# More Strassen pairs in an MLP's down projection, their weight-block sums made by DMA in two quarters of the residual

## The chip, the cores and the metric

The kernel runs on one core of a Trainium2 chip. Its time is the device time of one execution in microseconds (us); the figure compared is the median over several executions. One execution is also recorded by the hardware profiler, and its trace is what the views below are taken from.

## The reference

One block of an encoder, batch 1, 256 rows, width 2048, in float32. Four kinds of mixers, an output projection and a cross-attention stand ahead of the part that matters here:

```python
D_MODEL = 2048
SEQ = 256
D_FF = ((8 * D_MODEL // 3 + 255) // 256) * 256        # 5632

def swiglu(h, w_gate_up, w_down):
    gate, up = jnp.split(h @ w_gate_up, 2, axis=-1)
    return (jax.nn.silu(gate) * up) @ w_down

def reference(x, mem, norm_g, ...):
    ...
    for l in range(DEPTH):                             # DEPTH is 1
        ...
        x = x + mix @ w_out[l]
        x = x + cross_attention(rms_norm(x, norm_g[l, 1]), mem_n, w_xq[l], w_xkv[l], w_xo[l])
        x = x + swiglu(rms_norm(x, norm_g[l, 2]), w_gate_up[l], w_down[l])
    return rms_norm(x, final_norm_g)
```

## The kernel before

**Products.** Every float32 operand is held as two parts, hi and lo. A product of 128 rows of activations with a block row of 512 weight columns is three matmuls on TensorE (PE), hi with wh (L472), hi with wl (L473) and lo with wh (L474), all in `part`.

**Weights.** They stream from HBM in slabs of 16 blocks of 128x128, 1 MB each (`Stream`). `_load` reads a slab into one of three raw buffers; ScalarE (ACT) rounds a half of it to wh (L166, or L178 in a pair), and VectorE (DVE) subtracts to get wl (L167, L179). The halves lie in a ring of split buffers: three, with one more (`wy`) in the MLP, and another (`wz`) in most of gate_up. So Down has four, and a cast waits until PE has used up the half four places earlier. GpSimd (POOL) and SyncE (SP) issue DMAs. The order of these steps on ACT and DVE is fixed in the program by the order in which they are written (`add_manual_dep` in `_half`).

**Plain slabs and pairs.** The MLP's slabs go by plans, strings with one letter a slab. N is a plain slab: four steps of 512 columns, two row halves each, 24 matmuls. S and s are pairs: two k-blocks and two groups of 512 columns, in which Strassen's form does with seven products what takes eight, 21 matmuls. A pair needs sums of activations (`combine`, nine VectorE operations, and casts by ScalarE), and sums of the four weight blocks. The split is then made in four phases (`_sums`): a block pair, a single block, a block pair, a block pair. In a pair of kind s, VectorE makes the sums of weight blocks in the raw buffer with four operations of 128x512 between the second phase and the third (L189). In a pair of kind S, two of them are made by DMA: SP reads 256 KB into a tile t (L114), ScalarE copies it into t's second half (L119), and POOL adds 512 KB from HBM to t by an accumulating DMA (L121); VectorE then makes only two sums, and the raw buffer reads only 768 KB. The tiles t are the four quarters of the residual `res`, whose rows lie in HBM in the meantime (`leave`) and are read back at the end of gate_up. In the code before, only gate_up has pairs of kind S with DMA sums; Down writes S in its plans too, but its slabs aren't in `SUMMED`, so that they are made as s.

**gate_up** is a first group of columns without pairs and ten groups of eight slabs each (`GROUPS`). After every group, silu(gate) times up is stored to HBM by POOL (`hidden<-g`, L600) and read back turned (`tmp<-hidden`, L605); ScalarE and VectorE split it to the activations f[0] to f[43] of Down (`fetch`). 22 of them are fetched during gate_up, the others at its end and in Down.

**Down** runs two passes of 22 slabs (`PASSES`), each for two groups of 512 columns; the last three slabs of pass 2 (`LATE`) are held for `down_end`, which finishes the last columns and the final norm. `mixed` adds the four banks of the pairs to the residual when the last pair of a pass is done. `paired_rows` works the plain steps in the order of k, those in `soon` first; `ready(k)` makes sure that f[k] is there, with the number of tiles to be had rising by three in four steps; `before(j)` makes sure that the combine of the pair at j is there. Otherwise fetches and combines are written into the program from a queue (`Background`), by a modelled time of PE and VectorE.

Of the kernel before, what the change touches and what calls it, by code (L numbers as in the profile page):

```python
# [19 lines left out]
ALU = mybir.AluOpType  # L20
# [8 lines left out]
FT = DFF // P  # L29
# [10 lines left out]
ROWS = ((0, 512), (704, 1024), (1088, NBLK))  # L40

LATE = 12

GATE_UP = 1920 // 16 + 8
GROUPS = *["NSSNSSNN"] * 9, "NSNSNSNN"

DOWN = GATE_UP + 80
PASSES = "NNNNNSNNSNNSNSNNSNNSNN", "NSNSNSNSNSNSNSNSNSNNNN"

PAIRED = {a + i for a, plan in [(GATE_UP + 8 * j, GROUPS[j % len(GROUPS)]) for j in range(10)] + [(DOWN, PASSES[0]), (DOWN + 22, PASSES[1])]  # L50
          for i, x in enumerate(plan) if x in "Ss"}
AHEAD = (-3, -3)

SUMS = [{GATE_UP + 8 * j + i + a: GATE_UP + 8 * j + i for j in range(10) for i, x in enumerate(GROUPS[j % len(GROUPS)]) if x == "S"}
        for a in AHEAD]

SUMMED = {GATE_UP + 8 * j + i for j in range(10) for i, x in enumerate(GROUPS[j % len(GROUPS)]) if x == "S"}

LAG, OWED, SOON, FAR = 1.3, 0.9, 0.01, 18.0
V_NG = 0  # L60
# [16 lines left out]
class Stream:  # L77


    def __init__(self, tc, pools, W, bg):  # L80
        self.tc, self.nc, self.W, self.bg = tc, tc.nc, W, bg
        self.rawp, self.wp = pools
        self.order = []
        self.n = self.made = 0
        self.after = []
        self.halves = []
        self.at = self.phase = 0
        self.raw = None
        self.ring = [[self.wp, -1] for _ in range(3)]
        self.last = {}  # L90
        self.raws = [[self.rawp, -1] for _ in range(3)]
        self.sums = []
        self.places = []
        self.two = []
        self.begun = []

    def _buffers(self, n, m):

# [6 lines left out]
    def _load(self, n):  # L105

        nc = self.nc
        slot = min(self.raws, key=lambda x: x[1])
        slot[1] = n
        self.raw = slot[0].tile([P, 2048], F32, name="raw", tag="raw")  # L110
        if n // 16 in SUMS[0]:
            t = self.sums[0]
            self.sums.append(self.sums.pop(0))
            nc.sync.dma_start(t[:, 0:512], self.W[SUMS[0][n // 16]][:, 1536:2048])  # L114
            self.begun.append(t)
        if n // 16 in SUMS[1]:
            t = self.begun.pop(0)
            mark = len(nc.cur_bb.bb.instructions)
            nc.scalar.copy(t[:, 512:1024], t[:, 0:512])  # L119
            self.keep(mark)  # L120
            nc.gpsimd.dma_start(t, self.W[SUMS[1][n // 16]][:, 512:1536], accum_op=ALU.add)  # L121
            self.two.append(t)
        if n // 16 in SUMMED:
            nc.sync.dma_start(self.raw[:, 0:1536], self.W[n // 16][:, 0:1536])
            return
        for a, b in zip(CUTS[n], CUTS[n][1:]) if n in CUTS else [(0, 1024), (1024, 2048)] if self.after else [(0, 2048)]:
            (nc.scalar if (n, a) == (0, 0) else nc.sync).dma_start(self.raw[:, a:b], self.W[n // 16][:, a:b])
            if self.after:
                self.after.pop(0)()

    def _half(self):
# [5 lines left out]
        mark = len(ins)  # L137
        (self._sums if n // 16 in PAIRED else self._plain)()
        if n // 16 < GATE_UP - 12:
# [31 lines left out]
    def _sums(self):  # L171

        nc, r, ph = self.nc, self.raw, self.phase
        summed = self.made // 16 in SUMMED
        t = self.two and self.two[0]
# [55 lines left out]
    def take_sums(self, w, ks, cols):  # L231

        assert self.n // 16 in PAIRED and self.n % 16 == 0
        self.order += [(w, ks[k], cols[c] + i * P) for k, c in ((1, 0), (0, 0), (1, 1), (0, 1)) for i in range(4)]
# [58 lines left out]
class Block:  # L293
# [563 lines left out]
    def whole(self, c):  # L857
        return self.res[c].rearrange("p k r -> p (k r)")

    def leave(self, c):  # L860
        self.nc.sync.dma_start(self.rd[:, c * 1024:(c + 1) * 1024], self.whole(c))

# [237 lines left out]
    def gate_up(self, gp, f, z):  # L1100

        nc = self.nc
        box, g, stored = {}, {}, []
# [36 lines left out]
        def fetch(k0, k1, ahead, pause, after=0, slow=False):  # L1140

            m = {}
            for k in range(k0, k1 + ahead):
                if k < k1:
                    while len(stored) <= k // 4:
                        yield
                    while after and self.bg.now < stored[k // 4] + after:
                        yield
                    m[k] = self.tmp()
                    mark = self.mark()  # L1150
                    self.load_turned(m[k], self.ff, k)
                    self.keep_place(mark)
                    if slow and k < k0 + ahead - 1:
                        yield
                if k >= k0 + ahead:
                    while k0 == 0 and k - ahead >= 20 and "free" not in box:
                        yield
                    mark = self.mark()
                    self.split(f[k - ahead], m.pop(k - ahead))
                    self.keep_place(mark)  # L1160
                    self.have = k - ahead + 1
                    yield pause
# [21 lines left out]
        sums = [((2 * i, 2 * i + 1), z[(i + 1) % 4]) for i in range(4)]  # L1184
        comb = self.bg.add(combined())
        whole = [self.whole(c) for c in range(4)]
# [17 lines left out]
        self.st.raws.append([rx, -1])  # L1204
        gate(ps[0])
        up(0, ps[1])
        early = fetch(0, FT - 22, 2, 2.0, 12, True)
        self.bg.drain(comb)
        for j in range(1, DFF // 512):
            plan = GROUPS[(j - 1) % len(GROUPS)]  # L1210
            if j == 10:
                box["free"] = True
            turns = [i for i, x in enumerate(plan) if x == "N"][:3]
            if j == 10:
                rest = fetch(FT - 22, FT, 6, SOON, slow=True)

            def begin(i):

                if (j, i) == (10, 5):
                    self.st.back(self.wz, rx)  # L1220
                if i in turns:
                    next(early, None)
                if j == 10 and i > 2:
                    next(rest)

            upped(j, self.paired_rows("w_gate_up", [j * 512, DFF + j * 512], self.h3, sums[:8 - plan.count("N")], plan, mixed, gated,
                                      before=begin, swap=j % 2 == 0)[0])
        more.close()
        for c, x in enumerate(whole):
            nc.sync.dma_start(x, self.rd[:, c * 1024:(c + 1) * 1024])  # L1230
        for _ in early:
            pass
        self.fetch = self.bg.add(rest)
# [1 line left out]
    def down(self, f, sp):  # L1235
# [4 lines left out]
        nc, st = self.nc, self.st  # L1240
        ss = self.rp.tile([P, 24], F32, name="rc", tag="rc")
        self.gap(sp, 192)
        z = [sp.tile([P, 768], F32R, name=f"y{i}") for i in range(8)]
        u = sp.tile([P, 512], F32, name="u")
        sums = [((2 * i, 2 * i + 1), z[i % 8]) for i in range(PASSES[1].count("S"))]
        made, split = [], []

        def combined(n):
# [36 lines left out]
        asked = itertools.count(1)  # L1285

        def ready(k):

            need = min(FT, max(k + 3, FT - 22 + next(asked) * 3 // 4))
            while self.have < need:  # L1290
                self.bg.step(next(e for e in self.bg.q if e[0] is self.fetch))

        for i, plan in enumerate(PASSES):
            n = plan.count("S")
            g = self.bg.add(combined(n))
            late = (0, LATE)[i]
            plan = plan[:22 - late // 4]

            def before(j):
                while plan[j] == "S" and len(made) <= plan[:j].count("S"):  # L1300
                    self.bg.step(next(e for e in self.bg.q if e[0] is g))
                if late and j == len(plan) - 2:
                    st.back(self.wy)

            ps, rest = self.paired_rows("w_down", [2 * i * 512, (2 * i + 1) * 512], f, sums[:n], plan,
                                        lambda *q: mixed(2 * i, *q), lambda *q: done(2 * i, *q), ready, late, before, i == 1,
                                        () if i else range(2 * n, 2 * n + 8))
            if i == 0:
                done(1, *ps)
        return ss, ps, rest, split  # L1310
# [316 lines left out]
class Gla:  # L1627
# [31 lines left out]
    def fetch(self):  # L1659

        b = self.b
        for to, k in ((self.k, 2), (self.q, 0)):
            for hd in range(4):
                c = (k + hd // 2) * R
                src = b.gq[c:c + R, :].rearrange("(g f) (b t) -> (f b) g t", f=32, t=32)[hd % 2 * 64:hd % 2 * 64 + 64]
                for d in (0, 64):
                    b.nc.gpsimd.dma_start(to[d:d + 64, hd, :].rearrange("p (g t) -> p g t", t=32), src)
# [324 lines left out]
```

## Time and profile before

| | us |
|---|---|
| median of 3 runs | 1429.03 |
| fastest, slowest | 1428.62, 1430.32 |
| the profiled execution | 1428.43 |
| its span | 1426.6 |
| outside the span | 1.8 |
| Down starts (first f tile in a matmul) | about 1186 |
| pass 2 starts | about 1301 |

Line numbers in the views are those of the kernel before. PE is TensorE's matmuls, PEld its weight loads, DVE is VectorE, ACT ScalarE, POOL GpSimd, SP SyncE. A row of a timeline gives start, duration, engine, line, operation, output<-inputs with shapes and the number of operations put together (x); in brackets the idle time before it, and what ended it. A row of waits gives who waited for whom: total us, times, longest. The granted clock of TensorE was 0.999 over the span, so that nothing here is a matter of its throttle.

### The profile page before, as it was taken

How to read it: one execution, taken by the hardware profiler on the slowest of the kernel's cores; microseconds unless marked ns; L12 is line 12 of the kernel's file. 1: busy time of each engine (PE TensorE's matmuls, PEld its weight loads, DVE VectorE, ACT ScalarE, POOL GpSimd, SP SyncE). 2: the span in 40 equal slices, each digit the busy share in tenths (PEclk: the TensorE clock that was granted, in tenths of full speed). 3: DMA queues.
4: the chain of work that ended last, by engine and by line, in shares of the span. 5: the costliest groups of instructions: out<-in, count | busy, mean ns of one | idle time of the engine just before them, and what ended most of it. 6: DMA issues, size and time to landing. Idle time of an engine off the chain costs nothing.

```text
span 1426.6 us, 18663 instructions
## 1 busy us (share of the span) xinstructions
PE 1416.5 (99%) x6562; PEld 1176.1 (82%) x6562; DVE 1174.3 (82%) x1782; ACT 850.2 (60%) x1242; POOL 243.4 (17%) x315
## 2 busy tenths in 40 slices
PE   9999999999999999999999999999999999999997
PEld 8888888888888888888888888888888888788886
DVE  6667868787878767677578999999999988989997
ACT  7566665445755555555465676667666665655655
POOL 0000100003212233531331121122211024000000
PEclk9999999999999999999999999999999999999999
DMA  9886554457566797965798999999999898665554
GB/s 356 294 291 250 204 198 174 161 177 232 183 216 215 234 278 249 276 197 188 252 298 257 265 280 283 288 291 260 278 291 273 276 276 242 212 235 179 193 220 148
DMA packets 72462, 344.84 MB, mean 242 GB/s; under 512 B 10894, under 2 KB 12591, under 8 KB 45745
## 3 DMA queue, kind: packets, MB, share of 16 engines
q1 hardware_dynamic: 52976, 285.31, 57.4%
q0 software_dynamic: 18960, 57.69, 17.2%
q8 instruction: 51, 0.84, 0.2%
q10 hardware_dynamic: 432, 0.66, 0.1%
q14 instruction: 43, 0.34, 0.1%
HBM read 321.07 MB, written 22.54 MB: 241 GB/s over the span
## 4 chain that ended last, share of the span: by engine, by line
PE 92%; issue 3%; DVE 2%; DMA 2%; POOL 1%; ACT 0%; SPq 0%; DVEq 0%; ACTq 0%; POOLq 0%
PE pg L472 21%; PE pg L474 21%; PE pg L473 21%; PE pm L473 6%; PE pm L474 6%; PE pm L472 6%; PE pg L420 4%; PE pg L421 2%; PE pm L1445 1%; DMA raw<-in_W 1%; PE pm L1074 1%; DMA tmp<-hidden 1%; POOL tmp L605 1%; PE pm L1045 1%; DVE wl L179 0%
## 5 line engine op out<-in xcount | busy, mean ns | idle before, releaser
L167 DVE TENSOR_TENSOR wl<-raw,wh 128x1024 fp32r<-128x1024 f32 (+1 forms) x395 | 473.7, 1212 | 161.3 <-ACT wh L166 159.4
L166 ACT CAST wh<-raw 128x1024 fp32r<-128x1024 f32 (+1 forms) x395 | 406.4, 1042 | 253.0 <-PE pg L474 189.0
L472 PE MATMUL pg<-wh,act 128*128 128x512 f32 (+1 forms) x1165 | 455.5, 391 | 0.0
L474 PE MATMUL pg<-wh,act 128*128 128x512 f32 (+1 forms) x1165 | 453.9, 390 | 0.5 <-DVE act L322 0.5
L473 PE MATMUL pg<-wl,act 128*128 128x512 f32 (+1 forms) x1165 | 453.6, 389 | 0.2 <-DVE wl L167 0.2
L474 PEld LDWEIGHTS pg<-wh,act 128*128 128x128 f32 x1165 | 218.9, 188 | 47.0 <-DVE act L322 1.1
L472 PEld LDWEIGHTS pg<-wh,act 128*128 128x128 f32 x1165 | 219.0, 188 | 46.8 <-issue 1.5
L473 PEld LDWEIGHTS pg<-wl,act 128*128 128x128 f32 x1165 | 219.0, 188 | 45.1 <-DVE wl L167 0.5
L178 ACT CAST wh<-raw 128x1024 fp32r<-128x1024 f32 (+1 forms) x177 | 161.5, 918 | 158.8 <-DVE raw L189 62.7
L179 DVE TENSOR_TENSOR wl<-raw,wh 128x1024 fp32r<-128x1024 f32 (+1 forms) x177 | 182.7, 1057 | 25.7 <-ACT wh L178 24.3
L473 PE MATMUL pm<-wl,act 128*128 128x512 f32 x290 | 112.9, 389 | 0.2 <-DVE wl L167 0.2
L472 PE MATMUL pm<-wh,act 128*128 128x512 f32 x290 | 112.8, 389 | 0.0
L474 PE MATMUL pm<-wh,act 128*128 128x512 f32 x290 | 112.8, 389 | 0.0
L420 PE MATMUL pg<-act,wh 128*128 128x512 f32 x256 | 90.5, 395 | 0.0
L121 POOL DMA_DIRECT2D res<-in_W x39 | 35.0, 897 | 238.3 <-ACT res L119 211.1
L421 PE MATMUL pg<-act,wl 128*128 128x256 f32 x256 | 71.8, 280 | 0.0
L189 DVE TENSOR_TENSOR raw<-raw 128x512 f32<-128x512 f32 x99 | 68.2, 689 | 1.6
L473 PEld LDWEIGHTS pm<-wl,act 128*128 128x128 f32 x290 | 54.4, 188 | 11.8 <-DVE wl L167 0.5
L474 PEld LDWEIGHTS pm<-wh,act 128*128 128x128 f32 x290 | 54.4, 188 | 11.3
L472 PEld LDWEIGHTS pm<-wh,act 128*128 128x128 f32 x290 | 54.4, 188 | 11.3
L420 PEld LDWEIGHTS pg<-act,wh 128*128 128x128 f32 x256 | 48.1, 188 | 10.5
L178 ACT CAST wh<-res 128x1024 fp32r<-128x1024 f32 x39 | 41.2, 1055 | 14.8 <-PE pg L474 4.1
(376 smaller groups left out, 1933.0 us busy)
## 6 DMA issues: line engine op xcount, KB each, us to landing
raw<-in_W SPq DMA_DIRECT2D x207, 1024.0 KB, 5.5
raw<-in_W SPq DMA_DIRECT2D x39, 768.0 KB, 8.9
res<-in_W POOLq DMA_DIRECT2D x39, 512.0 KB, 9.7
res<-in_W SPq DMA_DIRECT2D x39, 256.0 KB, 4.9
raw<-in_W SPq DMA_DIRECT2D x11, 512.0 KB, 7.1
hidden<-g POOLq DMA_DIRECT2D x22, 256.0 KB, 4.0
tmp<-hidden POOLq DMA_DIRECT2D x44, 128.0 KB, 10.5
features<-tmp POOLq DMA_DIRECT2D x32, 128.0 KB, 4.6
```

Of the source, the lines that this page charges most:

```text
L121: nc.gpsimd.dma_start(t, self.W[SUMS[1][n // 16]][:, 512:1536], accum_op=ALU.add)
L166: nc.scalar.copy(wh[:, a:b], r[:, a:b])
L167: nc.vector.tensor_tensor(out=wl[:, a:b], in0=r[:, a:b], in1=wh[:, a:b].bitcast(F32), op=ALU.subtract)
L178: nc.scalar.copy(wh, src)
L179: nc.vector.tensor_tensor(out=wl, in0=src, in1=wh.bitcast(F32), op=ALU.subtract)
L189: nc.vector.tensor_tensor(out=out, in0=a, in1=b, op=ALU.add)
L420: self.nc.tensor.matmul(p[:, :], wh, slot[:, :], start=start, stop=False)
L421: self.nc.tensor.matmul(p[:, 0:R], wl, slot[:, 0:R], start=False, stop=stop)
L472: self.nc.tensor.matmul(p, hi, wh, start=start, stop=False)
L473: self.nc.tensor.matmul(p, hi, wl, start=False, stop=False)
L474: self.nc.tensor.matmul(p, lo, wh, start=False, stop=stop)
L605: self.nc.gpsimd.dma_start(t.rearrange("p (g t) -> p g t", t=32), src)
```

## The change

Down's pairs go from 6 to 8 in the first pass and from 9 to 11 in the second; 14 of these 19 get the sums by DMA (S), into two tiles, the quarters 2 and 3 of the residual; 5 of pass 2 keep VectorE's sums (s). The last group of gate_up gets a fourth pair. When the DMAs of a pair begin is worked out in `begins`: three slabs ahead, or in the slab behind the tile's last user. Quarters 0 and 1 of the residual are read back at the end of gate_up as before, 2 and 3 two slabs behind the last S of pass 2. 20 tiles f are fetched in gate_up instead of 22 (`EARLY`), since the fourth pair uses the place of two of them, and the order of Down's first plain steps starts with four tiles (16 to 19) instead of eight (12 to 19). The five more pairs have 15 matmuls fewer than the slabs that they replace.

```diff
+EARLY = 20
-GROUPS = *["NSSNSSNN"] * 9, "NSNSNSNN"
+GROUPS = "NSSNSSNN",
-PASSES = "NNNNNSNNSNNSNSNNSNNSNN", "NSNSNSNSNSNSNSNSNSNNNN"
...
-AHEAD = (-3, -3)
-SUMS = [{GATE_UP + 8 * j + i + a: GATE_UP + 8 * j + i for j in range(10) for i, x in enumerate(GROUPS[j % len(GROUPS)]) if x == "S"}
-        for a in AHEAD]
-SUMMED = {GATE_UP + 8 * j + i for j in range(10) for i, x in enumerate(GROUPS[j % len(GROUPS)]) if x == "S"}
+PASSES = "NNNNNSNSNSNSNSNSNSNSNN", "NSsNSsNSNSsNSNSNssNNNN"
+...
+PAIRED, SUMMED = ({a + i for a, plan in PLANS for i, x in enumerate(plan) if x in kinds} for kinds in ("Ss", "S"))
+def begins():
+    at = {}
+    for ns, tiles in (([n for n in sorted(SUMMED) if n < DOWN], 4), ([n for n in sorted(SUMMED) if n >= DOWN], 2)):
+        for i, n in enumerate(ns):
+            a = max(n - 3, ns[i - tiles] + 1) if i >= tiles else n - 3
+            assert a not in at and a < n, (a, n)
+            at[a] = n
+    return at
+SUMS = begins()
...
-        if n // 16 in SUMS[0]:
+        if n // 16 in SUMS:
             t = self.sums[0]
             self.sums.append(self.sums.pop(0))
-            nc.sync.dma_start(t[:, 0:512], self.W[SUMS[0][n // 16]][:, 1536:2048])
-            self.begun.append(t)
-        if n // 16 in SUMS[1]:
-            t = self.begun.pop(0)
+            nc.sync.dma_start(t[:, 0:512], self.W[SUMS[n // 16]][:, 1536:2048])
             mark = len(nc.cur_bb.bb.instructions)
             nc.scalar.copy(t[:, 512:1024], t[:, 0:512])
             self.keep(mark)
-            nc.gpsimd.dma_start(t, self.W[SUMS[1][n // 16]][:, 512:1536], accum_op=ALU.add)
+            nc.gpsimd.dma_start(t, self.W[SUMS[n // 16]][:, 512:1536], accum_op=ALU.add)
...
+    def fetch_rows(self, cs):
+        for c in cs:
+            self.nc.sync.dma_start(self.whole(c), self.rd[:, c * 1024:(c + 1) * 1024])
...
-                    while k0 == 0 and k - ahead >= 20 and "free" not in box:
-                        yield
...
-        early = fetch(0, FT - 22, 2, 2.0, 12, True)
+        early = fetch(0, EARLY, 2, 2.0, 12, True)
...
-                rest = fetch(FT - 22, FT, 6, SOON, slow=True)
+                rest = fetch(EARLY, FT, 6, SOON, slow=True)
...
-        for c, x in enumerate(whole):
-            nc.sync.dma_start(x, self.rd[:, c * 1024:(c + 1) * 1024])
+        self.fetch_rows((0, 1))
+        self.st.sums = whole[2:]
...
-            need = min(FT, max(k + 3, FT - 22 + next(asked) * 3 // 4))
+            need = min(FT, max(k + 3, EARLY + next(asked) * 3 // 4))
...
+                if i and j == plan.rindex("S") + 2:
+                    self.fetch_rows((2, 3))
...
-                                        () if i else range(2 * n, 2 * n + 8))
+                                        () if i else range(2 * n, EARLY))
```

More of the change, by code (lines that the diff above doesn't have):

```diff
@@ L42 @@
 LATE = 12
+EARLY = 20
 GATE_UP = 1920 // 16 + 8
-GROUPS = *["NSSNSSNN"] * 9, "NSNSNSNN"
+GROUPS = "NSSNSSNN",
 DOWN = GATE_UP + 80
-PASSES = "NNNNNSNNSNNSNSNNSNNSNN", "NSNSNSNSNSNSNSNSNSNNNN"
-PAIRED = {a + i for a, plan in [(GATE_UP + 8 * j, GROUPS[j % len(GROUPS)]) for j in range(10)] + [(DOWN, PASSES[0]), (DOWN + 22, PASSES[1])]
-          for i, x in enumerate(plan) if x in "Ss"}
-AHEAD = (-3, -3)
-SUMS = [{GATE_UP + 8 * j + i + a: GATE_UP + 8 * j + i for j in range(10) for i, x in enumerate(GROUPS[j % len(GROUPS)]) if x == "S"}
-        for a in AHEAD]
-SUMMED = {GATE_UP + 8 * j + i for j in range(10) for i, x in enumerate(GROUPS[j % len(GROUPS)]) if x == "S"}
+PASSES = "NNNNNSNSNSNSNSNSNSNSNN", "NSsNSsNSNSsNSNSNssNNNN"
+PLANS = [(GATE_UP + 8 * j, GROUPS[j % len(GROUPS)]) for j in range(10)] + [(DOWN, PASSES[0]), (DOWN + 22, PASSES[1])]
+PAIRED, SUMMED = ({a + i for a, plan in PLANS for i, x in enumerate(plan) if x in kinds} for kinds in ("Ss", "S"))
[8 more added lines that the diff above has]
+SUMS = begins()
 LAG, OWED, SOON, FAR = 1.3, 0.9, 0.01, 18.0
@@ L94, in __init__ @@
         self.two = []
-        self.begun = []
     def _buffers(self, n, m):
@@ L1210, in gate_up @@
             plan = GROUPS[(j - 1) % len(GROUPS)]
-            if j == 10:
-                box["free"] = True
             turns = [i for i, x in enumerate(plan) if x == "N"][:3]
             if j == 10:
-                rest = fetch(FT - 22, FT, 6, SOON, slow=True)
+                rest = fetch(EARLY, FT, 6, SOON, slow=True)
             def begin(i):
@@ L1244, in down @@
         u = sp.tile([P, 512], F32, name="u")
-        sums = [((2 * i, 2 * i + 1), z[i % 8]) for i in range(PASSES[1].count("S"))]
+        sums = [((2 * i, 2 * i + 1), z[i % 8]) for i in range(sum(x in "Ss" for x in PASSES[1]))]
         made, split = [], []
@@ L1293, in down @@
         for i, plan in enumerate(PASSES):
-            n = plan.count("S")
+            n = sum(x in "Ss" for x in plan)
             g = self.bg.add(combined(n))
@@ L1299, in before @@
             def before(j):
-                while plan[j] == "S" and len(made) <= plan[:j].count("S"):
+                while plan[j] in "Ss" and len(made) <= sum(x in "Ss" for x in plan[:j]):
                     self.bg.step(next(e for e in self.bg.q if e[0] is g))
+                if i and j == plan.rindex("S") + 2:
+                    self.fetch_rows((2, 3))
                 if late and j == len(plan) - 2:
```

## The prediction

> **What bounds the kernel now.** I read the page from the top: busy shares, slices, the chain that ended last.
>
> ```profile
> span 1426.6 us, 18663 instructions
> ...
> PE 1416.5 (99%) x6562; PEld 1176.1 (82%) x6562; DVE 1174.3 (82%) x1782; ACT 850.2 (60%) x1242; POOL 243.4 (17%) x315
> ...
> DVE  6667868787878767677578999999999988989997
> ...
> PE 92%; issue 3%; DVE 2%; DMA 2%; POOL 1%; ACT 0%; SPq 0%; DVEq 0%; ACTq 0%; POOLq 0%
> ```
>
> TensorE is busy 99% and carries 92% of the chain: the time is its matmuls plus the few places where it stands. But VectorE's slices are at 8 and 9 through the MLP, where the change is. Next, PE's waits from the end of gate_up to the end of the kernel, and busy time by stretch: f tiles arriving, the pairs of pass 1, pass 2, the end.
>
> ```profile
> PE pg L474 <- DVE act L322: 0.5, 1, 0.5
> PE pm L472 <- ACT y L338: 0.2, 1, 0.2
> PE pm L473 <- DVE wl L167: 0.2, 1, 0.2
> ```
>
> ```profile
> core 0: us, PE busy (x) PEld busy (x) DVE busy (x) ACT busy (x) POOL busy (x), PEclk, DMA share, GB/s
> 1186.00:1213.60 27.60, 27.60 (x123) 22.87 (x122) 22.85 (x37) 14.96 (x25) 15.57 (x18) 1.00 0.89 243
> 1213.60:1302.00 88.40, 87.67 (x385) 71.86 (x384) 82.67 (x139) 52.81 (x75) 0.88 (x1) 1.00 0.58 204
> 1302.00:1395.00 93.00, 93.00 (x411) 76.74 (x410) 88.81 (x124) 55.16 (x70) 0.00 (x0) 1.00 0.55 201
> ```
>
> Down loses 0.9 us in three waits. It has nothing to win but matmuls, and it runs VectorE at 82.67 of 88.40 (94%) and 88.81 of 93.00 (95%). So the question is how little slack there is half by half. Pass 2 gives PE's rate: 93.00/411 = 0.2263 us a matmul. A plain slab (24) is 5.43 us, a pair (21) 4.75, half a plain slab (12) 2.72.
>
> **1. Fewer matmuls.** Pairs go 6 to 8, 9 to 11 and 3 to 4, five more, each with 21 matmuls for 24. 15 x 0.2263 = **-3.4**, certain, since PE is the path throughout.
>
> **2. The three waits of before.** Their neighbourhoods change; taken as gone, **-0.9** (bounds -0.9 and 0).
>
> **3. Pairs that follow a pair (pass 2).** Before, a plain slab stood between any two pairs. After, an s (its four sums of weight blocks on VectorE) follows an S three times, and an s another s once. The steady period of pass 2 shows what the half behind a pair has to spare: ScalarE's casts, VectorE's operations, and PE's first two matmuls on that half (start, duration).
>
> ```profile
> 1380.53 1.05 ACT L178 CAST wh<-raw 128x1024 fp32r<-128x1024 f32 x1 [1.17 <-PE pm L474]
> 1381.89 2.00 ACT L166 CAST wh<-raw 128x1024 fp32r<-128x1024 f32 x2 [0.31 <-PE pm L474]
> ```
>
> ```profile
> 1382.97 2.36 DVE L167 TENSOR_TENSOR wl<-raw,wh 128x1024 fp32r<-128x1024 f32 x2
> 1385.25 1.82 DVE L179 TENSOR_TENSOR wl<-raw,wh 128x1024 fp32r<-128x1024 f32 x2
> 1386.99 2.87 DVE L189 TENSOR_TENSOR raw<-raw 128x512 f32<-128x512 f32 x4
> 1389.77 1.22 DVE L179 TENSOR_TENSOR wl<-raw,wh 128x1024 fp32r<-128x1024 f32 x1
> ```
>
> ```profile
> 1385.05 0.39 PE L472 MATMUL pm<-wh,z 128*128 128x512 f32 x1
> 1385.28 0.39 PE L473 MATMUL pm<-wl,z 128*128 128x512 f32 x1
> ```
>
> The cast behind the pair (1381.89) waits for PE: with four split buffers it can't be earlier, whatever VectorE has free. Its wl starts at 1382.97 and is ready about 1.2 later; the first matmul that reads it starts at 1385.28. The lead is 2.31 - 1.2 = 1.1. A plain half gives PE 12 matmuls, and the lead holds. Let that half be the first phase of an s instead. From the start of the first phase's wl to the end of the third's is 1390.99 - 1385.25 = 5.74 (split, half split, four sums, split), so the third is ready at 1382.97 + 5.74 = 1388.71. PE has only 9 matmuls before it (2.04) and wants it at 1387.32: 1.4 late. Low end 0.6 an occurrence: three matmuls of the third phase need only wh and stand before the wait in part. High end 2: pieces of a combine (2.2 us, below) fall in between. Four times 1.4 = **+5.6** (2.4 to 8). An S behind a pair is cheaper (two sums, 1.39, instead of four) and none stands there.
>
> **4. End of pass 2.** The mixing of the four banks of products now comes behind two pairs in a row, in VectorE's queue ahead of the splits of the last plain slabs: **+0.9** (0 to 2), a third of the 2.72 us that PE works on a half.
>
> **5. Pass 1's alternation.** It now runs NS eight times where three plain slabs in five stood. VectorE's costs:
>
> ```profile
> 1214.57 0.69 DVE L322 TENSOR_TENSOR tmp<-tmp 128x128 f32<-128x128 f32 x3
> ...
> 1218.39 0.75 DVE L322 TENSOR_TENSOR tmp<-act 128x256 f32<-128x256 f32 x2
> ...
> 1233.66 4.63 DVE L167 TENSOR_TENSOR wl<-raw,wh 128x1024 fp32r<-128x1024 f32 x4
> ```
>
> In a run each operation costs less than its own duration: a split of 1024 (4.63 - 1.22)/3 = 1.14 (1.22 is the single one at 1389.77), 128 columns 0.2, 256 columns 0.33, a sum of 512 0.70 ((1389.77 - 1386.99)/4), a split of 512 about 0.6 (1.82 - 1.22). A combine is three of 256 and six of 128: 2.2. So N+S takes VectorE 5 x 1.14 + 0.6 + 2 x 0.70 + 2.2 = 9.9, against 5.43 + 4.75 = 10.2 on PE. It just fits, but an estimated twelve f tiles are split (0.33 each) in the first three and a half periods: 38.6 against 35.6, 3.0 over, of which the lead saves a little: **+2.5** (0 if VectorE spends idle time ahead of the first pair; 6 if each of the eight pairs loses 0.75).
>
> The Trainium skill, page "VectorE: DVE Perf Modes", section "The DRAIN you can't avoid", says that the next operation does not start until the pipe is empty. By that rule four splits would take 4 x 1.22 = 4.9 and N+S at least 5 x 0.08 = 0.4 more, 10.3 against 10.2 (an estimate), so that each of the eight periods would run over; the 4.63 of the row disagrees, and the measurement decides.
>
> **6. The DMA's sums of weight blocks.** Fourteen S of Down get the round trip that gate_up's 39 had: 256 KB into t by SP, a copy by ScalarE, 512 KB accumulated by POOL's queue. Rows of gate_up: the landing times of the first and of the second DMA by source line, the groups of the POOL issues and of the copies, and a stretch of gate_up with its DMA share.
>
> ```profile
> DMA to landing us min/median/max: 2.9/4.9/11.1
> ```
>
> ```profile
> DMA to landing us min/median/max: 5.8/9.7/14.0
> ```
>
> ```profile
> L121 POOL DMA_DIRECT2D res<-in_W x39 | 35.0, 897 | 238.3 <-ACT res L119 211.1
> ...
> L119 ACT COPY res<-res 128x512 f32<-128x512 f32 x39 | 23.9, 614 | 0.0
> ```
>
> ```profile
> 800.00:1000.00 200.00, 200.00 (x884) 165.62 (x883) 192.43 (x234) 134.44 (x169) 40.34 (x46) 1.00 0.93 278
> ```
>
> Down's two tiles are two of the residual's quarters, and t of the next S but one is begun one slab after the tile's last reader. From that reading to the need PE works through about 18.4 us (1.36 of the pair, N, S, N and 1.4 of the next pair: 1.36 + 5.43 + 4.75 + 5.43 + 1.4); the trip is 4.9 + 0.6 + 0.9 (POOL's issue) + 9.7 = 16.1 by medians. It fits by 2.3, and Down's DMA share of 0.55 to 0.58, against 0.93, speaks for the faster half. What shows is the copy: in ScalarE's queue it is ahead of the next slab's first cast. At slab 6 of pass 1 this cast must wait until t, whose DMA waits for the last reading at slab 5, has landed: 2.9 + 0.6 + cast 1.05 + split 1.2 = 5.8 after that reading, where PE needs it after its lead (two halves, 2.2, with only plain slabs before) and 12 matmuls (2.7): **+0.9** (0 with more lead; 2.9 with the median landing). At slabs 8 to 16 the copy stands behind one or two casts already wanted, and nothing is late. SP's queue: raw's DMA is issued behind t's, but its buffer is free only after the same slab's last split. POOL's queue is under 7.
>
> The Trainium skill, page "DMA: Bandwidth & Descriptors", section "Anatomy of one DMA — SWDGE (gpsimd) path", gives 2.0 us plus the bytes at 436 GB/s: an estimate of 2.6 and 3.2 us here. By it this step would come to 0.6 and round trips could never be late; the medians of 4.9 and 9.7 disagree, and I go by them.
>
> **7. Hidden tiles needed earlier.** f20 to f43 are asked for at Down's third slab instead of the fifth, the later ones up to 16 us earlier.
>
> ```profile
> 1189.69 1.52 POOL L600 DMA_DIRECT2D hidden<-g  x2 [33.32 <-DVE g L598]
> 1191.20 7.03 POOL L605 DMA_DIRECT2D tmp<-hidden  x8
> 1198.90 2.63 POOL L605 DMA_DIRECT2D tmp<-hidden  x3 [0.67 <-DMA tmp<-hidden]
> ```
>
> ```profile
> 1205.71 0.41 ACT L330 CAST act<-tmp 128x256 fp32r<-128x256 f32 x1 [0.84 <-DMA tmp<-hidden]
> ```
>
> The loads come eight deep, ScalarE already waits for one (0.84), and now two accumulating DMAs of 512 KB stand among them in POOL's queue (0.9 each to issue): **+1.0** (0 to 4; 4 when a tile comes half a slab and the two issues late).
>
> At nothing: the fourth pair of the last gate_up group, where the ring still has five split buffers, one more than in item 3 (cover gone: 1.4); the fetching of two quarters of the residual only after the last S, since `mixed` needs them more than a slab later and 4.9 covers a landing (cover gone: its excess over 5.43).
>
> **The sum.** -3.4 - 0.9 + 5.6 + 0.9 + 2.5 + 0.9 + 1.0 = +6.6 on the profiled execution's 1428.43 (span 1426.6 and 1.8 around it): 1435.0. That execution lies 0.6 under the median of 1429.03, so **1435.5**. 0.2%, about what a measurement here can tell from no change, is 2.9 us: 1426.2 to 1431.9 is the same.
>
> **Rivals.** *Faster (0.17).* VectorE's relief takes up the waits: pass 2 has 5 pairs with four sums and 6 with two, 32 sums for 36, and 95% busy is not 100%. If casts behind a pair find their lead, only items 1 and 2 show: 1429.03 - 4.3 = 1424.7. For it: before, PE lost 0.9 us in all of Down. Against it: the cast that PE itself releases (1381.89) can't be moved by relief.
>
> *The same (0.15).* The four places cost the low end of 0.6 and pass 1 fits: -4.3 + 2.4 + 0.9 = -1.0: 1428. For it: the 9.9 against 10.2 of item 5.
>
> *Round trips late (0.15), slower still.* With two tiles a trip above 18.4 us stops the third phase of its pair. One with both DMAs at the maxima is 11.1 + 0.6 + 0.9 + 14.0 = 26.6. It decides once landings exceed the medians by 2.3 together. If six of the trips are 1.4 over: 1435.5 + 8.4 = 1443.9. Against it: the DMA share of Down.
>
> That the change doesn't do what it says is no case: the plans fix the number of matmuls.
>
> **How the numbers follow.** The forecast case (1432 to 1441) gets the remaining 0.53: **1435.5**. The range reaches to the faster case and nearly to the late trips, and leaves out their outer halves: 1424.5 to 1443.5. Faster 0.17, same 0.15, slower 0.53 + 0.15 = 0.68.
>
> **What would show it.** 15 fewer matmuls at an unchanged 0.2263. In pass 2, PE waits for wl (L179) at the third phase of the four s behind pairs, about 1.4 each, and VectorE without idle time there. In pass 1, a wait for wh at slab 6, ScalarE's copy just before; waits for wl at alternate slabs; early in Down a wait for a tile from hidden. Items 3 to 7 are wrong if PE stands less than 2 us in Down; item 6 if PE or VectorE waits for res from DMA.

## The result and the profile after

| | before | after |
|---|---|---|
| median, us | 1429.18 (1428.62 to 1430.32) | 1443.01 (1442.59 to 1443.98) |
| ratio | | 1.0097 (95%: 1.0079 to 1.0114) |
| profiled execution, span | 1428.43, 1426.6 | 1443.98, 1442.2 |

The change costs 13.8 us, where 6.5 was forecast. In the kernel after, the lines that matter stand five further down: the three matmuls are L477, L478 and L479, the casts L171 and L183, the splits L172 and L184, the sums L194, the copy L124, the accumulating DMA L126 and the loads of hidden L610.

The page of the kernel after:

```profile
span 1442.2 us, 18792 instructions
...
PE 1419.9 (98%) x6547; PEld 1171.7 (81%) x6547; DVE 1181.5 (82%) x1800; ACT 865.6 (60%) x1273; POOL 256.1 (18%) x330
...
DVE  6677868777977667676669999999999996999987
...
PE 88%; DVE 4%; DMA 3%; issue 2%; ACT 1%; POOL 0%; SPq 0%; ACTq 0%; DVEq 0%; POOLq 0%
```

The matmuls fell by 15 (6562 to 6547). PE's part of the chain fell from 92% to 88%, and VectorE, DMA and ScalarE came in. VectorE's slices show a 6 at Down's start (the slice from 1190 to 1226): there it stood as well, so it wasn't VectorE alone that ran out. PE's waits name the places:

```profile
PE pg L477 <- DMA tmp<-hidden: 4.0, 1, 4.0
PE pm L477 <- ACT wh L183: 3.7, 4, 1.0
PE pg L478 <- DVE wl L172: 1.6, 5, 0.5
PE pg L477 <- ACT wh L171: 1.3, 2, 0.7
...
PE pg L477 <- ACT wh L183: 0.9, 3, 0.3
PE pm L1353 <- ACT tmp L343: 0.9, 1, 0.9
```

There is one long wait for a tile from hidden, there are four waits of 0.7 to 1.0 for the cast in a pair, and the rest is small. PE's timeline at the long wait:

```profile
1214.76 0.39 PE L479 MATMUL pg<-wh,act 128*128 128x512 f32 x1
1219.18 0.53 PE L477 MATMUL pg<-wh,act 128*128 128x512 f32 x1 [4.03 <-DMA tmp<-hidden]
...
1220.80 0.63 PE L479 MATMUL pm<-wh,y 128*128 128x512 f32 x1
1221.23 0.63 PE L477 MATMUL pm<-wh,y 128*128 128x512 f32 x1
1221.66 0.63 PE L479 MATMUL pg<-wh,act 128*128 128x512 f32 x1
```

After the stop, matmuls start every 0.43 instead of 0.227. The granted clock says the same: 0.75 over the 6.90 us of the next row (start and end of a stretch, length, busy us and count of each engine, granted clock, DMA share, GB/s; the rows after it are the rest of pass 1, and pass 2):

```profile
1219.10:1226.00 6.90, 6.36 (x20) 4.61 (x21) 3.15 (x4) 3.49 (x6) 2.54 (x4) 0.75 0.90 226
```

```profile
1226.00:1302.00 76.00, 74.43 (x316) 58.13 (x315) 73.12 (x130) 51.63 (x81) 6.24 (x8) 1.00 0.82 235
1302.00:1410.00 108.00, 103.22 (x445) 82.50 (x444) 99.78 (x140) 64.51 (x84) 4.25 (x5) 1.00 0.71 225
```

Where PE doesn't wait, matmuls start every 0.2267 us (the mean from 800 to 1000, before and after). The time lost is what the count doesn't explain: 76.0 - 316 x 0.2267 = 4.4 in the rest of pass 1 (before, in the same stretch, 0.5 with 333 matmuls), and 108.0 - 445 x 0.2267 = 7.1 in pass 2 (before 0, from 1302 to 1395). From 1214.76 to 1226, adding what the intervals between matmul starts exceed 0.227, it is 6.6: 4.3 of the stop, 1.6 of the slow clock, 0.7 of the wait behind it. The end of Down lost 1.8 instead of 0.7. Together, 6.6 + 4.4 + 7.1 + 1.8 = 19.9, less 1.8 of before (0.6 in one wait at 1215.7, 0.5 and 0.7), less 3.4 for the matmuls, is 14.7 of the 15.6 between the two spans; 0.7 of the rest was there at the 300th matmul already, far from the change.

**Why the tile came late.** POOL's timeline at Down's start, after:

```profile
1189.16 0.93 POOL L126 DMA_DIRECT2D res<-in_W  x1 [32.81 <-ACT res L124]
1189.75 1.89 POOL L605 DMA_DIRECT2D hidden<-g  x2
1191.25 5.67 POOL L610 DMA_DIRECT2D tmp<-hidden  x6
...
1199.56 0.88 POOL L610 DMA_DIRECT2D tmp<-hidden  x1 [1.49 <-DMA hidden<-g]
1200.94 0.88 POOL L610 DMA_DIRECT2D tmp<-hidden  x1 [0.49 <-DMA tmp<-hidden]
1204.89 0.93 POOL L126 DMA_DIRECT2D res<-in_W  x1 [3.07 <-ACT res L124]
1205.48 6.53 POOL L610 DMA_DIRECT2D tmp<-hidden  x7
1223.45 0.91 POOL L126 DMA_DIRECT2D res<-in_W  x1 [11.45 <-ACT res L124]
1224.05 3.02 POOL L610 DMA_DIRECT2D tmp<-hidden  x3
```

Before, eleven loads were issued by 1201.5 (the two rows of step 7). Here the tenth waits until 1205.48: the accumulating DMA of slab 7's pair (1204.89) stands ahead of it in POOL's queue, and that waits 3.07 for ScalarE's copy. ScalarE in turn had stood for the first tiles:

```profile
1200.24 0.41 ACT L335 CAST z<-tmp 128x256 fp32r<-128x256 f32 x1 [4.41 <-DMA tmp<-hidden]
...
1203.97 0.62 ACT L124 COPY res<-res 128x512 f32<-128x512 f32 x1
...
1217.07 0.40 ACT L335 CAST act<-tmp 128x256 fp32r<-128x256 f32 x1 [4.91 <-DMA tmp<-hidden]
...
1222.54 0.62 ACT L124 COPY res<-res 128x512 f32<-128x512 f32 x1 [3.41 <-DMA res<-in_W]
```

So two queues, each in order, wait for each other: loads stand behind a DMA that waits for a copy that stands behind casts that wait for loads. The tile that PE wants at 1215 is the tenth load, issued at 1205.48, right behind the DMA that waited, and landed at 1217.05; its cast, its split, a combine that reads it and the combine's cast take the 2.1 us from there to PE's matmul. In the run `e5_first_s` below, without that DMA, the tenth load is issued at 1199.94 and lands at 1211.51: it takes 11.57 from issue to landing in both, so that the 5.5 by which the tile is late are all in the issue. Of these, 1.9 were there at the ninth load already (1200.94 for 1199.07); the hold of 3.07 and the DMA's own issue are the rest. The last row is the copy of step 6, ahead of slab 6's first cast. The other accumulating DMA, of slab 5 (1189.16), is ahead of the last stores to hidden.

**A pair behind a pair.** At the first of the four places, where an s stands behind an S, the rows are ScalarE's, then VectorE's, then PE's:

```profile
1323.62 1.05 ACT L183 CAST wh<-raw 128x1024 fp32r<-128x1024 f32 x1 [0.19 <-DVE raw L194]
...
1325.39 1.04 ACT L183 CAST wh<-raw 128x1024 fp32r<-128x1024 f32 x1 [0.52 <-DVE raw L194]
```

```profile
1322.05 0.69 DVE L194 TENSOR_TENSOR raw<-raw 128x512 f32<-128x512 f32 x1
1322.65 0.28 DVE L327 TENSOR_TENSOR tmp<-tmp 128x128 f32<-128x128 f32 x1
1322.85 0.69 DVE L194 TENSOR_TENSOR raw<-raw 128x512 f32<-128x512 f32 x1
...
1324.59 0.68 DVE L194 TENSOR_TENSOR raw<-raw 128x512 f32<-128x512 f32 x1
1325.19 1.22 DVE L184 TENSOR_TENSOR wl<-raw,wh 128x1024 fp32r<-128x1024 f32 x1
```

```profile
1324.01 0.39 PE L479 MATMUL pm<-wh,act 128*128 128x512 f32 x1
1324.72 0.73 PE L477 MATMUL pg<-wh,y 128*128 128x512 f32 x2 [0.33 <-ACT wh L183]
1326.48 0.50 PE L477 MATMUL pm<-wh,act 128*128 128x512 f32 x1 [1.03 <-ACT wh L183]
1326.82 0.40 PE L478 MATMUL pg<-wl,y 128*128 128x512 f32 x1
```

PE waits first for the third phase's cast, then, after the two matmuls that need only wh, for the fourth's, which reads the last of the four sums. A combine's pieces (L327) stand between the sums. About 1.9 is lost here.

### The profile page after: what moved, and what is told of

It is laid out like the page before. It is cut to its first block, busy times and chain, and to the rows that moved or that the text cites. A ratio compares the mean times of both kernels' runs of the same rounds, so it can differ in the third digit from the quotient of the medians.

```text
span 1442.2 us, 18792 instructions
## 1 busy us (share of the span) xinstructions
PE 1419.9 (98%) x6547; PEld 1171.7 (81%) x6547; DVE 1181.5 (82%) x1800; ACT 865.6 (60%) x1273; POOL 256.1 (18%) x330
## 4 chain that ended last, share of the span: by engine, by line
PE 88%; DVE 4%; DMA 3%; issue 2%; ACT 1%; POOL 0%; SPq 0%; ACTq 0%; DVEq 0%; POOLq 0%
PE pg L478 20%; PE pg L479 20%; PE pg L477 20%; PE pm L477 6%; PE pm L478 6%; PE pm L479 6%; PE pg L425 4%; PE pg L426 2%; DVE wl L184 2%; DMA res<-in_W 1%; DVE raw L194 1%; DMA raw<-in_W 1%; PE pm L1453 1%; PE pm L1084 1%; DMA tmp<-hidden 1%
## 5 line engine op out<-in xcount | busy, mean ns | idle before, releaser
L172 DVE TENSOR_TENSOR wl<-raw,wh 128x1024 fp32r<-128x1024 f32 (+1 forms) x385 | 462.3, 1212 | 162.5 <-ACT wh L171 158.3
L171 ACT CAST wh<-raw 128x1024 fp32r<-128x1024 f32 (+1 forms) x385 | 396.1, 1042 | 247.0 <-PE pg L479 181.7
L477 PE MATMUL pg<-wh,act 128*128 128x512 f32 (+1 forms) x1166 | 455.9, 391 | 5.4 <-DMA tmp<-hidden 4.0
L478 PE MATMUL pg<-wl,act 128*128 128x512 f32 (+1 forms) x1166 | 454.4, 390 | 1.2 <-DVE wl L172 1.1
L479 PE MATMUL pg<-wh,act 128*128 128x512 f32 (+1 forms) x1166 | 453.7, 390 | 0.0
L477 PEld LDWEIGHTS pg<-wh,act 128*128 128x128 f32 x1166 | 218.9, 188 | 53.8 <-ACT act L343 5.0
L478 PEld LDWEIGHTS pg<-wl,act 128*128 128x128 f32 x1166 | 219.0, 188 | 47.5 <-DVE wl L172 3.1
L479 PEld LDWEIGHTS pg<-wh,act 128*128 128x128 f32 x1166 | 218.9, 188 | 46.1 <-DVE act L327 0.2
L183 ACT CAST wh<-raw 128x1024 fp32r<-128x1024 f32 (+1 forms) x182 | 163.1, 908 | 138.0 <-DVE raw L194 47.1
L184 DVE TENSOR_TENSOR wl<-raw,wh 128x1024 fp32r<-128x1024 f32 (+1 forms) x182 | 185.4, 1047 | 27.7 <-ACT wh L183 26.0
L126 POOL DMA_DIRECT2D res<-in_W x54 | 47.6, 882 | 415.9 <-ACT res L124 354.4
L477 PE MATMUL pm<-wh,act 128*128 128x512 f32 x284 | 110.5, 390 | 2.0 <-ACT wh L183 2.0
L478 PE MATMUL pm<-wl,act 128*128 128x512 f32 x284 | 110.8, 390 | 0.2 <-DVE wl L172 0.2
L479 PE MATMUL pm<-wh,act 128*128 128x512 f32 x284 | 110.5, 389 | 0.0
L183 ACT CAST wh<-res 128x1024 fp32r<-128x1024 f32 x54 | 57.0, 1055 | 27.5 <-PE pm L479 9.1
L184 DVE TENSOR_TENSOR wl<-res,wh 128x1024 fp32r<-128x1024 f32 x54 | 65.6, 1215 | 0.7 <-ACT wh L183 0.7
L477 PEld LDWEIGHTS pm<-wh,act 128*128 128x128 f32 x284 | 53.3, 188 | 14.1 <-ACT wh L183 2.9
L478 PEld LDWEIGHTS pm<-wl,act 128*128 128x128 f32 x284 | 53.3, 188 | 12.1 <-DVE wl L172 1.0
L479 PEld LDWEIGHTS pm<-wh,act 128*128 128x128 f32 x284 | 53.3, 188 | 11.0
```

The lines of the kernel that those rows point to most:

```text
L126: nc.gpsimd.dma_start(t, self.W[SUMS[n // 16]][:, 512:1536], accum_op=ALU.add)
L171: nc.scalar.copy(wh[:, a:b], r[:, a:b])
L172: nc.vector.tensor_tensor(out=wl[:, a:b], in0=r[:, a:b], in1=wh[:, a:b].bitcast(F32), op=ALU.subtract)
L183: nc.scalar.copy(wh, src)
L184: nc.vector.tensor_tensor(out=wl, in0=src, in1=wh.bitcast(F32), op=ALU.subtract)
L477: self.nc.tensor.matmul(p, hi, wh, start=start, stop=False)
```

## The experiments

Times are medians, beside those of the kernel before on the same chip (1428.67 to 1429.02); after the change it is 1443.01.

**The fourth pair of gate_up and 20 early tiles alone** (`e1_old_down`).

```diff
-PASSES = "NNNNNSNSNSNSNSNSNSNSNN", "NSsNSsNSNSsNSNSNssNNNN"
+PASSES = "NNNNNsNNsNNsNsNNsNNsNN", "NsNsNsNsNsNsNsNsNsNNNN"
-                if i and j == plan.rindex("S") + 2:
+                if i and j == 2:
```

> Only the fourth pair of gate_up's last group and the 20 tiles fetched early; Down has the pairs of the kernel before, all sums of weight blocks on VectorE. Theory A (from the trace after: the loss lies in Down, where the accumulating DMAs hold up the loads of hidden tiles, and where pairs stand behind pairs): -0.7 for three matmuls fewer, no long stall, 1428 to 1430. Theory B (20 instead of 22 tiles fetched early is what makes the tiles late): the stall at Down's start is here too, some 5 us, 1433 to 1436.

Measured 1429.75 (1.0007, 0.9998 to 1.0016): no long stall, so the loss is in Down's plans. But the three matmuls saved (0.7) don't show: PE waits once 1.0 for a hidden tile (L479 on VectorE's L327) where it was 0.5, and 0.8 for its splits where it was 0.2. I take it that the two tiles fetched later take back what the pair gives; no run has the one without the other.

**Down's plans alone** (`e2_down_only`): the last group of gate_up and the gate of the 22 tiles as before.

```diff
-EARLY = 20
-GROUPS = "NSSNSSNN",
+EARLY = 22
+GROUPS = *["NSSNSSNN"] * 9, "NSNSNSNN"
+                    while k0 == 0 and k - ahead >= 20 and "free" not in box:
+                        yield
+            if j == 10:
+                box["free"] = True
```

> Only Down's plans with the DMA's sums; gate_up's last group keeps three pairs and 22 tiles are fetched early. Theory A: two loads fewer come behind the accumulating DMA, the stall at Down's start gets shorter but stays at 2 us or more, and the four places in pass 2 (7.1 us together) are as they were: 1439 to 1443. Theory B: the stall of 4 us and the slow clock behind it are gone: 1436 to 1438.

Measured 1443.50 (1.0103, 1.0088 to 1.0118). The long wait is there, 5.0 us, with slow clock behind it; the four places are unchanged. The number of early tiles is not the cause. The expectation that the wait would get shorter was wrong.

**Pass 2 without adjacent pairs** (`e4_alternate`).

```diff
-PASSES = "NNNNNSNSNSNSNSNSNSNSNN", "NSsNSsNSNSsNSNSNssNNNN"
+PASSES = "NNNNNSNSNSNSNSNSNSNSNN", "NSNSNSNSNSNSNSNsNsNNNN"
```

> Pass 2 with 9 pairs that alternate with plain slabs (seven with the DMA's sums, two on VectorE) instead of 11 with four pairs directly behind pairs; six more matmuls, +1.4. Theory A (a pair behind a pair costs 1.4 to 1.9 in PE's waits): the waits of 7.1 at the four places go, 1443.0 - 7.1 + 1.4 = 1437.3, and pass 2 has less than 1 us of waits. Theory C (the DMA's load in Down is what slows the splits, wherever the pairs stand): pass 2 keeps 4 us or more of waits, 1441 to 1444.

Measured 1436.81 (1.0055, 1.0040 to 1.0070), 6.2 under the kernel after the change, with two pairs fewer. Its PE waits have next to nothing left of pass 2:

```profile
PE pg L477 <- ACT act L343: 4.5, 1, 4.5
...
PE pg L477 <- ACT wh L171: 0.6, 1, 0.6
PE pg L478 <- DVE wl L172: 0.6, 2, 0.5
PE pm L478 <- DVE wl L184: 0.2, 1, 0.2
```

The seven pairs with DMA sums that are left in pass 2 leave next to no wait there, so theory C falls. The long wait is still there, 4.5.

**The first two pairs of pass 1 on VectorE** (`e5_first_s`).

```diff
-PASSES = "NNNNNSNSNSNSNSNSNSNSNN", ...
+PASSES = "NNNNNsNsNSNSNSNSNSNSNN", ...
```

> The first two pairs of pass 1 get their sums of weight blocks from VectorE, so that no accumulating DMA stands among the loads of hidden tiles. Theory A: the loads are issued 3 us or more earlier, the stall of 4.2 and the slow clock behind it (1.6) go, and ScalarE's copy is no longer ahead of slab 6's cast; two pairs cost VectorE 1.4 each more: 1436 to 1439. Theory B (tiles are asked for too early): the stall stays at 3 us or more, 1442 to 1446.

Measured 1440.40 (1.0084, 1.0067 to 1.0101): a gain of 2.6, less than expected, though the stall and the slow clock are gone. POOL's loads, and the row of the pass from 1225 to 1240:

```profile
1191.03 7.02 POOL L610 DMA_DIRECT2D tmp<-hidden  x8
1199.07 1.75 POOL L610 DMA_DIRECT2D tmp<-hidden  x2 [1.02 <-DMA tmp<-hidden]
```

```profile
1225.00:1240.00 15.00, 12.87 (x54) 9.57 (x53) 14.83 (x30) 10.17 (x18) 0.92 (x1) 1.00 0.74 215
```

The tenth load goes at about 1200 instead of 1205.5. But PE loses 15.0 - 54 x 0.2267 = 2.8 in the 15 us of that row. VectorE is busy 14.83 there; it was busy 14.85 after the change and 14.97 before, and PE got through 58 and 65 matmuls. So VectorE is full in that stretch in all three, and I take it that what differs is its work for a matmul: pairs by turns with plain slabs, four sums a pair, and tiles to split.

**One of the two at a time** (`e10_only_second_s`: slab 5 S, slab 7 s; `e11_only_first_s`: slab 5 s, slab 7 S).

```diff
-PASSES = "NNNNNSNSNSNSNSNSNSNSNN", ...
+PASSES = "NNNNNSNsNSNSNSNSNSNSNN", ...     # e10
+PASSES = "NNNNNsNSNSNSNSNSNSNSNN", ...     # e11
```

> As after the change, but the pair at slab 7 of pass 1 is an s: the accumulating DMA of slab 5, ahead of the last stores of hidden, stays; the one that stood among the loads goes. Theory A3 (POOL's queue, held 3.07 us by the accumulating DMA of slab 7, made the tile late): the long stall goes, waits in the first 50 us of Down under 4 us and no slow clock there, 1437 to 1440. Theory A4 (the DMA of slab 5, which moves while hidden is stored and loaded, makes it late): the stall stays at 3 us or more, 1442 to 1445.

> The other half: the pair at slab 5 is an s, that at slab 7 keeps the DMA's sums. Theory A3: the stall stays at 3 us or more, 1442 to 1445. Theory A4: it goes, 1437 to 1440.

Measured 1442.75 (1.0098, 1.0083 to 1.0114) and 1441.87 (1.0093, 1.0079 to 1.0107). Neither theory holds alone: the stop is 2.0 us with only slab 5's DMA (and a slow clock behind it), 1.9 and 0.8 with only slab 7's (no slow clock), 4.2 with both, 0.8 with neither. How slab 5's acts is seen in the last stores to hidden, in e10_only_second_s and then in e11_only_first_s (the last number is the median from issue to landing):

```profile
hidden<-g POOLq DMA_DIRECT2D x2, 256.0 KB, 8.6
```

```profile
hidden<-g POOLq DMA_DIRECT2D x2, 256.0 KB, 4.3
```

With an accumulating DMA ahead in the same queue the last stores take 4.3 longer, and the loads that read them wait. Whether they wait for their place in the queue or for the bytes that move beside them no run shows. Slab 7's acts by its place among the loads: POOL is held 3.07 for the copy after the change, 1.77 in e11.

**The same bytes by SP** (`e7_traffic`), added to e5_first_s:

```diff
+        if n // 16 in (DOWN + 2, DOWN + 4):
+            t = self.sums[0]
+            self.sums.append(self.sums.pop(0))
+            nc.sync.dma_start(t, self.W[n // 16][:, 512:1536])
```

> The kernel with the first two pairs of pass 1 on VectorE (e5_first_s), with the 512 KB that each of the two accumulating DMAs moved read again, by SP as a plain load into the same free quarters at the same two slabs (data that nobody uses): the DMA load at Down's start is as after the change, POOL's queue is not held. Theory A (the loads were held in POOL's queue): no long stall, within 1.5 of e5_first_s, 1439 to 1442. Theory C (bandwidth): a stall of 3 us or more at Down's start and the slow clock behind it, 1444 to 1447.

Measured 1441.37 (1.0085, 1.0071 to 1.0099), 1.0 over e5_first_s, with no long stall: the longest single wait is 1.1. But the run doesn't put the bytes where it was meant to. SP's queue was ahead of POOL's, and the two loads (L131) were issued early:

```profile
1165.04 0.33 SPq L131 DMA_DIRECT2D res<-in_W  x1
...
1172.25 0.34 SPq L131 DMA_DIRECT2D res<-in_W  x1
```

The first landed 6.7 us later, and the second had landed when SP's next DMA into its tile went at 1179.69. So both were over before Down began, where after the change the accumulating DMAs moved from 1189.16 to 1194.78 and from 1204.89 to 1215.11. This run doesn't settle the rival of bandwidth, then. Against it, for slab 7's DMA, speaks the tenth load with its 11.57 us from issue to landing, with and without that DMA beside it; in e11_only_first_s it took 13.3, so there a part of the bytes isn't excluded. The run did get a slow clock, after waits that leave PE 36 and 48 matmuls in these two stretches:

```profile
1215.00:1225.00 10.00, 8.56 (x36) 6.10 (x35) 8.57 (x17) 5.99 (x11) 3.63 (x4) 1.00 1.02 260
1225.00:1240.00 15.00, 12.91 (x48) 9.59 (x47) 13.87 (x27) 9.10 (x15) 0.92 (x1) 0.89 0.77 215
```

**Slab 7's t begun a slab earlier** (`e13_begin_earlier`).

```diff
-            a = max(n - 3, ns[i - tiles] + 1) if i >= tiles else n - 3
+            a = max(n - 3, ns[i - tiles] + 1) if i >= tiles else n - 3 - (n == DOWN + 7)
```

> As after the change, but t of slab 7 is begun one slab earlier, at slab 3, in the second of the two free tiles. Theory A3: the accumulating DMA is further ahead in POOL's queue, fewer loads stand behind it; it still waits for ScalarE's copy, which stands behind casts that wait for loads: the stall falls from 4 to 1 to 3 us, 1439 to 1442. Theory A4: no change, 1442 to 1444.

Measured 1442.82 (1.0098, 1.0084 to 1.0111): the first stop falls to 2.8, with the same 3.4 us of slow clock, but a later wait grows from 0.6 to 1.6 (slab 6's cast, behind the copy of slab 9's t). No gain in sum: moving the DMA in the queue moves the wait.

**s before S** (`e6_swapped`).

```diff
-..., "NSsNSsNSNSsNSNSNssNNNN"
+..., "NsSNsSNsSNsSNSNSNsNNNN"
```

> Pass 2 has the same 11 pairs with the same 6 S and 5 s, but the three directly adjacent Ss become sS, and a fourth sS takes the place of the last ss: the second of two adjacent pairs is then an S, whose third phase needs no sum of VectorE. Theory A1 (a pair behind a pair waits because the four sums stand between its splits): the waits of 7.1 us at the four places fall under 1.5 in all, 1437 to 1438.5. Theory A2 (four split buffers are too few behind any pair, whatever kind follows): 5 us or more of waits stay there, 1441 to 1444.

Measured 1441.06 (1.0082, 1.0069 to 1.0096). The loss in pass 2 falls from 7.1 to 5.0 (93.0 - 388 x 0.2267, from 1302 to 1395). Theory A1 fails: it said under 1.5. The time and the waits lie at the low edge of theory A2's ranges:

```profile
PE pg L477 <- ACT wh L183: 2.1, 4, 0.7
...
PE pg L478 <- DVE wl L184: 0.9, 2, 0.6
```

ScalarE's cast for the fourth phase of the S still waits for its two sums (L194), behind splits that VectorE makes without a pause. So the order of the kinds is only a part of the price. Whether the rest is VectorE's time for two pairs or the four split buffers, as A2 has it, is open: no run has a fifth buffer.

**Fewer pairs, away from the loads** (`e8_seven_nine`, `e12_eight_nine`, `e9_seven_eleven`): gate_up as before, by the edit of e2_down_only, and these plans.

```diff
+PASSES = "NNNNNsNNsNNSNSNSNSNSNN", "NSNSNSNSNSNSNSNsNsNNNN"   # e8
+PASSES = "NNNNNsNNsNSNSNSNSNSNSN", "NSNSNSNSNSNSNSNsNsNNNN"   # e12
+PASSES = "NNNNNsNNsNNSNSNSNSNSNN", "NsSNsSNsSNsSNSNSNsNNNN"   # e9
```

> gate_up and its 22 tiles as before; pass 1 with 7 pairs, the first two on VectorE (at slabs 5 and 8), the DMA's sums only from slab 11 on, when all hidden tiles are loaded; pass 2 with 9 alternating pairs, seven with the DMA's sums. Theory A (only the three places found cost anything): one pair more than before and no new stall, -0.7 and 0.5 to 1 of ScalarE's copies: 1428 to 1429.5. Rival D (the round trips themselves disturb the splits, by DMA load or ScalarE's copies): 1431 to 1434.

> As e8_seven_nine with an eighth pair in pass 1 (slabs 5 and 8 on VectorE, 10 to 20 by twos with the DMA's sums): three matmuls fewer, -0.7 against e8_seven_nine. If the alternation costs nothing once the hidden tiles are in: 1428.5 to 1429.5; if a place short of VectorE's time remains: 1430 to 1432.

> As e8_seven_nine, with the 11 pairs of e6_swapped in pass 2, so three pairs more than the kernel before (9 matmuls, -2.0). Theory A1: 1427 to 1428.5. Theory A2: 1431 to 1434.

Measured 1429.63 (1.0003, 0.9994 to 1.0012), 1431.96 (1.0021, 1.0012 to 1.0029) and 1433.96 (1.0034, 1.0022 to 1.0046). With DMA sums away from the loads and no pair behind a pair, 12 of 16 pairs' sums leave no long wait, and the kernel is as fast as before, with a pair more; it is not faster. Its pass 2:

```profile
1302.00:1395.00 93.00, 93.00 (x412) 77.02 (x411) 79.70 (x101) 56.92 (x72) 4.25 (x5) 1.00 0.78 244
```

VectorE's 88.81 of 93.00 became 79.70 with PE at 93.00: the DMA's sums do what they are meant to, but PE did not wait for VectorE before. The eighth pair of e12 loses 1.4 in one wait, at the first pair of pass 2: its splits and sums stand in VectorE's queue behind the mixing of pass 1, whose last pair is now one slab from the end. The 11 pairs of e9 lose at the kind of places where e6 does.

## Why the prediction was right and wrong

The sign, the bound (PE, with waits taking the place of the matmuls saved) and most places were right. That the measured 13.8 lies inside the range is luck in part: it is about twice the 6.5 forecast (6.6 as the sum of the steps), and the range reached so high for the late round trips, which did not decide. Step by step, in us lost against the kernel before:

| step | forecast | measured |
|---|---|---|
| 1 matmuls | -3.4 | -3.4 (15 fewer) |
| 2 waits of before | -0.9 | -0.6 (the one at 1215.7); the others are in their stretches |
| 3 pair behind a pair | +5.6 | +7.1 (e4: all of it goes) |
| 4 end of pass 2 | +0.9 | +1.0 in the one profile, not by its cause |
| 5 alternation in pass 1 | +2.5 | +3.9 (4.4 less 0.5) |
| 6 copy at slab 6 | +0.9 | +0.7 (the wait ending at 1225.42) |
| 7 hidden tiles | +1.0 | +5.9 (4.3 and 1.6 of clock) |

**The step that failed is 7**, hidden tiles needed earlier: 5.9 for 1.0. With its forecast in place of its measured size the change would have cost 8.9. It was costed as two issues of 0.9 and half a slab of lateness, at most 4. It saw that the accumulating DMAs stand among the loads in POOL's queue, and did not ask what each of them waits for. The page before had it: POOL's 211.1 us of idle time at the accumulating DMA end with ScalarE's copy. In gate_up PE waited for no hidden tile. In Down the loads that PE needs stand behind it, and the copy stands in ScalarE's queue behind casts that wait for loads. The second half, that stores behind an accumulating DMA land after 8.6 instead of 4.3 (e10, e11), was in no term, nor was the slow clock.

**Step 3** named the four places, the third phase and the sums, and was 1.5 short over all: it followed the third phase alone, and the fourth waits for the last sums as well, with a combine's pieces between; 1.4 became 1.4 to 2.1. That an S behind a pair is cheaper held (e6), but only from 1.8 to 1.3 a place.

**Step 4** was wrong in its cause: the end lost 1.0 more in this one profile, at the matmuls that add the residual (L1353, waiting 0.9 for ScalarE), and e2, e4, e5 and e6 have 0.2 there, e8 0.8 with no pairs in a row. So it doesn't go with pairs in a row; why it is in some profiles is open.

**Step 5** was mis-sized, 3.9 for 2.5. The waits lie before 1271, in the first four periods or so. I take it that part of it is that slabs after the stop start without a lead; it can't be all, since e5, without the stop, loses 2.8 from 1225 to 1240. The step sets the 1.14 of a split against the Trainium skill, page "VectorE: DVE Perf Modes", section "The DRAIN you can't avoid". They aren't at odds: the same section goes on that a next operation that is not held starts earlier.

**Step 6** held in its number, and that is luck: the landing took 6.8 (issued 1215.7, copy at 1222.54), not the 2.9 that the step goes by, and the lead was larger, since PE had stood. The figure of the Trainium skill, page "DMA: Bandwidth & Descriptors", section "Anatomy of one DMA — SWDGE (gpsimd) path", 2.0 us and the bytes, is for DMAs that POOL issues: the 2.6 that the forecast drew from it for SP's, and with it the 0.6 for this step, aren't the page's. For POOL's the estimate of 3.2 is again far under what POOL's queue gave (the last number is the median to landing, for 512 KB):

```profile
res<-in_W POOLq DMA_DIRECT2D x54, 512.0 KB, 9.7
```

**The rivals.** Late round trips did not decide: the waits for t are ScalarE's, and only the one at slab 6 reached PE. The faster case fails at step 3: e8 has VectorE relieved by 9 us in pass 2 and gains nothing, and in the kernel after the change the waits stay where ScalarE's cast waits for a sum.

## What to carry to other kernels

When a DMA goes into an engine's in-order queue, cost what it waits for, not its issue alone, and list what stands behind it; if that leads back through a second queue to the first, the wait feeds itself. An engine at 95% that makes nobody wait was worth nothing to relieve here (e8), and one place where a pair follows a pair cost more (1.8) than a pair saves (0.7). Where PE may stop for a few us, add the slow clock that can come behind the stop (1.6 here).

## What the runs showed of the hardware

TensorE's clock fell to half for 3.4 us after the stop of 4.2 (intervals of 0.43 at 1220.80 and after). In other profiles of this study it fell for about 3.4 or 6.8: after a stop of 5.2 (e2), 5.0 (e6) or 4.7 (e4), but also after one of 2.8 (e13) or 2.0 (e10), while e11, with stops of 1.9 and 0.8, kept its clock; and in e7 after a few waits of 0.7 to 1.2 close together, while e5, with nearly the same waits, kept it. The Trainium skill, page "TensorE: Matmul & The Clock Gate", section "What's actually happening", tells of a free-running window of 3.4 us, and of half the clock after at least one idle window. The lengths agree, and e5 and e7 fit a window that doesn't start with the kernel; that the window must be idle does not agree: stops of 2.0 and 2.8 (e10, e13), shorter than the window, and the waits of e7 were enough.
